# Encoder layer on one core: left operands one piece a round, whole-round weight tiles, a shared subtraction, and a last product in two groups

## The chip, the cores and the metric

One core of a Trainium2 chip runs the whole layer in one launch. The metric is the device time in microseconds (us). The kernel before took 2439.3 us (median of 3 runs, 2437.79 to 2443.6); a measurement of this kernel can tell about 0.3% (7.3 us) from no change.

## What is computed

Two request groups go through one encoder layer with shared weights: the prompt (512 tokens) and the sample (1024 tokens), both of width 1024. Attention and cross-attention are not touched by the change. What is touched is the MLP and the last layer norm:

```python
def squared_relu_mlp(x, w_up, w_down):
    return jnp.square(jax.nn.relu(x @ w_up)) @ w_down
...
        x = layer_norm(ALPHA * x + squared_relu_mlp(x, w_up[l], w_down[l]), ln3_g[l], ln3_b[l])
```

w_up is 1024 x 4096 and w_down 4096 x 1024, all in float32.

## The kernel before

Every float32 product is made of three matmuls in the reduced format F32R: an operand is split into a high part (a cast on ACT) and a low part (the operand minus its high part, a subtraction on POOL or DVE), and high·high, high·low and low·high are summed in one PSUM bank (`mm3`, L128 to L130). A matmul here is 128x128 by 128x512.

The MLP runs in three stages, in this order of time.

The prompt's MLP (1372 to 1772 us of the span) has 32 rounds f. A round makes 128 columns of w_up (`col_block`) and 128 rows of w_down (`down_weights`) into parts, makes 24 matmuls for the hidden block (`up`: ReLU on ACT, square on DVE at L901, cast on ACT, low part on DVE at L904) and 24 for the down product (`down`), whose eight results DVE adds to the tokens (L925). Raw weights come in quarters, 128x512 each, through two shared buffers of the tag `wraw`; their parts lie in three buffers each of the tags `wh` and `wl`. In rounds 3 to 9 a whole call `left(i)` follows the round's own work: it makes one left operand of the sample's MLP, in four pieces k. A piece is an optional sum or difference (DVE, L883), a cast (ACT, L886), a subtraction (DVE, L887) and a store of 512 KB to the DRAM buffer `sa` (L888), through two buffers of the tag `kv`.

The sample's MLP computes each of its two matrix products as a two-by-two block product with seven products in place of eight (`PRODUCTS`: left operand, right operand, and the output blocks to which the result is added or subtracted). The up stage (1772 to 2086 us) runs the seven in the order `UP`, each with 16 blocks f of 12 matmuls; `left_load` brings a left operand back from `sa` (tags qt and pt, or gb and kv); `right` makes the right operand: loads into the tag `q` (seven buffers of 128x528), a sum on DVE (L960) where there are two, a cast on ACT (L963), the subtraction on POOL (L964). DVE adds the results to the hidden blocks (L1001) and squares them (L950). The down stage (2086 us to the end) runs the seven in the order `DOWN`, 16 chunks c of 12 matmuls each (L1045 to L1047, four token tiles by three): the left operand is a hidden block or a sum of two (DVE, L1037), cast on ACT (L1040), subtracted on DVE (L1041); the right operand is `right` with the subtraction on DVE. After a product DVE adds its four banks to the outputs `accs` (L1055, L1057: "collects"). `finish(h)` runs the layer norm on the four token tiles of a half and stores them (L1028): the first half when product 1 is collected, beside the last product, the second half at the end.

In `layer_norm`, L151 and L152 are the statistics, L155 a power on POOL, L159 the first multiplication on DVE. With `spread` 1 both halves of a tile go on with a scaling on ACT (L166) and an addition on POOL (L170); with `spread` 2 the first half is done on DVE (L164) and the second on ACT and DVE (L166, L168).

Each engine works through its own list in order, and so does the queue SP, which issues every DMA. The order of the lists is drawn up when the kernel is built, by the tile framework's planner from program order, buffers and its own estimates, so an instruction may stand earlier in a list than its line says. Buffers of a tag go round in program order.

Of the kernel before, what the change touches and what calls it, by code (L numbers as in the profile page):

```python
# [12 lines left out]
F32 = mybir.dt.float32  # L13
# [7 lines left out]
D = 1024  # L21
# [10 lines left out]
def f32(ap):  # L32
    return ap.bitcast(F32)
# [3 lines left out]
def tile_encoder_layer(ctx: ExitStack, tc: tile.TileContext, d, outs):  # L37
# [109 lines left out]
    def layer_norm(x, g, b, spread=0):  # L147


        st = sb.tile([P, 16], F32, name="lnst", bufs=2)  # L150
        V.bn_stats(st[:, 0:6], x[:, 0:512])  # L151
        V.bn_stats(st[:, 6:12], x[:, 512:1024])  # L152
# [720 lines left out]
    UP, DOWN = (5, 3, 2, 4, 1, 7, 6), (3, 5, 4, 2, 7, 1, 6)  # L873


    def left(i):
        blk = lambda b, k: X2[1 + b[0]][:, 4 * b[1] + k]
        what = PRODUCTS[i][0]
        for k in range(4):
            x = blk(what[0], k)  # L880
            if len(what) > 1:
                y = slot("cpr")
                V.tensor_tensor(y, x, blk(what[2], k), op=what[1])  # L883
                x = y
            t = slot("kv", dt=F32R)
            A.activation(t[:, 0:512], x, AF.Copy)  # L886
            V.tensor_sub(t[:, 512:1024], x, f32(t[:, 0:512]))  # L887
            S.dma_start(sa[i - 1][k], f32(t).rearrange("p (j c) -> p j c", j=2))  # L888
# [65 lines left out]
    def right(what, load, low, tag=None):  # L954
# [7 lines left out]
        t = wp.tile([P, 1024], F32R, name="wh", tag=tag or ("wh", "wl")[next(ring) % 2])  # L962
        A.activation(t[:, 0:512], x, AF.Copy)  # L963
        low.tensor_sub(t[:, 512:1024], x, f32(t[:, 0:512]))  # L964
        return t[:, 0:512], t[:, 512:1024]
# [56 lines left out]
    g3 = None  # L1022

    def finish(h):
        for t in range(4):
            layer_norm(accs[h][t], [g3[:, 0], g3[:, 1]], [g3[:, 2], g3[:, 3]], 1 if t % 2 else 2)
            row = 512 * h + t * P
            S.dma_start(outs[1][0, row:row + P], accs[h][t])  # L1028

    for n, i in enumerate(DOWN):  # L1030
        lw, rw, into = PRODUCTS[i]
        banks = [bank(tag) for tag in (("pj", "pj", "s", "s") if n % 2 == 0 else ("t", "t", "t", "o"))]
        for c in range(16):
            x = hidden(lw[0], c)
            if len(lw) > 1:
                y = wp.tile([P, 512], F32, name="wraw", tag="wraw", bufs=2)
                V.tensor_tensor(y, x, hidden(lw[2], c), op=lw[1])  # L1037
                x = y
            a = wp.tile([P, 1024], F32R, name="wh", tag="wh")
            A.activation(a[:, 0:512], x, AF.Copy)  # L1040
            V.tensor_sub(a[:, 512:1024], x, f32(a[:, 0:512]))  # L1041
            rh, rl = right(rw, down_block(c), V, "wl")
            for t in range(4):
                lh, ll = a[:, t * P:(t + 1) * P], a[:, 512 + t * P:512 + (t + 1) * P]
                T.matmul(banks[t], lh, rh, start=(c == 0), stop=False)  # L1045
                T.matmul(banks[t], lh, rl, start=False, stop=False)  # L1046
                T.matmul(banks[t], ll, rh, start=False, stop=(c == 15))  # L1047
            if n == 0:
                square((1, 1), c)
        for t in range(4):  # L1050
            for b, op in into:
                x = accs[b[0]][t][:, b[1] * 512:(b[1] + 1) * 512]
                if (b, t) not in done:
                    done.add((b, t))
                    V.scalar_tensor_tensor(x, x, ALPHA, banks[t], op0=ALU.mult, op1=op)  # L1055
                else:
                    V.tensor_tensor(x, x, banks[t], op=op)  # L1057
        if i == 7:
            g3 = act.tile([P, 8, 512], F32, name="g3", tag="act")
            for j, name in enumerate(("ln3_g", "ln3_b")):  # L1060
                src = d[name][0]
                S.dma_start(g3[:, 2 * j:2 * j + 2].rearrange("p a c -> p (a c)"),
                            bass.AP(tensor=src.tensor, offset=src.offset, ap=[[0, P], [1, D]]))
        if i == 1:
            finish(0)
    finish(1)


# [62 lines left out]
```

## Time and profile before

| | us |
|---|---|
| median of 3 runs | 2439.3 |
| lowest, highest run | 2437.79, 2443.6 |
| the profiled execution's own time | 2432.93 |
| its span in the trace | 2431.2 |

| engine | busy us | share of the span |
|---|---|---|
| PE (matmul) | 2321.2 | 95% |
| DVE | 1667.1 | 69% |
| ACT | 1034.1 | 43% |
| POOL | 910.0 | 37% |

A matmul's busy time is modelled and matmuls overlap, so the rows are read by the number of matmuls in a stretch and by the pauses between them. Durations of DVE operations overlap a little too: what counts is from start to start.

### The profile page before, as it was taken

How to read it: one execution, taken by the hardware profiler on the slowest of the kernel's cores; microseconds unless marked ns; L12 is line 12 of the kernel's file. 1: busy time of each engine (PE TensorE's matmuls, PEld its weight loads, DVE VectorE, ACT ScalarE, POOL GpSimd, SP SyncE). 2: the span in 40 equal slices, each digit the busy share in tenths (PEclk: the TensorE clock that was granted, in tenths of full speed). 3: DMA queues.
4: the chain of work that ended last, by engine and by line, in shares of the span. 5: the costliest groups of instructions: out<-in, count | busy, mean ns of one | idle time of the engine just before them, and what ended most of it. 6: DMA issues, size and time to landing. Idle time of an engine off the chain costs nothing.

```text
span 2431.2 us, 33241 instructions
## 1 busy us (share of the span) xinstructions
PE 2321.2 (95%) x11128; PEld 1916.6 (79%) x11128; DVE 1667.1 (69%) x3294; ACT 1034.1 (43%) x2181; POOL 910.0 (37%) x798
## 2 busy tenths in 40 slices
PE   8989999999999999999989989999999999999995
PEld 6868778898888787778878876788888877888873
DVE  6266545666656776658576679666655799887997
ACT  4346644666545634434233334333354222344432
POOL 7555442121234125333244444454475445100013
PEclk9999999999999999999999999999999999999998
DMA  9676345444444543435325366433376677634553
GB/s 323 199 191 174 85 119 131 118 115 101 94 119 116 168 130 104 139 113 173 108 92 188 101 205 242 131 98 93 100 242 180 192 240 219 208 125 147 189 170 119
DMA packets 394043, 371.00 MB, mean 153 GB/s; under 512 B 72976, under 2 KB 302352, under 8 KB 393872
## 3 DMA queue, kind: packets, MB, share of 16 engines
q1 hardware_dynamic: 393872, 368.88, 50.7%
q8 instruction: 88, 1.44, 0.2%
q14 instruction: 83, 0.68, 0.1%
HBM read 290.75 MB, written 52.97 MB: 141 GB/s over the span
## 4 chain that ended last, share of the span: by engine, by line
PE 38%; DVE 9%; DMA 4%; issue 3%; POOL 2%; ACT 1%; POOLq 0%; SPq 0%; DVEq 0%; ACTq 0%
PE pj L128 5%; PE pj L129 5%; PE pj L130 5%; DVE cpr L960 2%; PE s L128 2%; PE s L130 2%; PE s L129 2%; PE t L128 2%; PE t L130 2%; PE t L129 2%; PE t L1045 1%; PE t L1046 1%; PE t L1047 1%; DVE h L1001 1%; DMA q<-in_w_up_dram 1%
## 5 line engine op out<-in xcount | busy, mean ns | idle before, releaser
L106 POOL TENSOR_TENSOR wl<-wraw,wh 128x512 fp32r<-128x512 f32 x144 | 196.6, 1378 | 262.8 <-ACT wh L105 240.3
L960 DVE TENSOR_TENSOR cpr<-q 128x512 f32<-128x512 f32 x160 | 148.8, 931 | 47.4 <-DMA q<-in_w_up_dram 19.2
L155 POOL TENSOR_TENSOR lnst<-lnst,mhalf 128x1 f32<-128x1 f32 x48 | 51.6, 1078 | 342.5 <-DVE lnst L154 339.6
L432 ACT ACTIVATE q<-q,st 128x256 f32<-128x256 f32 (+3 forms) x256 | 138.2, 545 | 74.9 <-DVE st L431 72.0
L963 ACT ACTIVATE wh<-cpr 128x512 fp32r<-128x512 f32 x160 | 100.3, 627 | 161.5 <-DVE cpr L960 140.2
L105 ACT ACTIVATE wh<-wraw 128x512 fp32r<-128x512 f32 x144 | 87.9, 629 | 182.3 <-DMA wraw<-in_w_up_dram 50.3
L478 DVE TENSOR_TENSOR pt<-t,pt 128x512 fp32r<-128x512 f32 x160 | 105.4, 671 | 86.5 <-ACT pt L477 85.9
L964 POOL TENSOR_TENSOR wh<-cpr,wh 128x512 fp32r<-128x512 f32 x80 | 114.4, 1431 | 115.7 <-ACT wh L963 115.7
L296 POOL TENSOR_TENSOR wl<-wraw,wh 128x256 fp32r<-128x256 f32 x128 | 95.5, 771 | 153.5 <-ACT wh L295 141.8
L912 POOL TENSOR_TENSOR wl<-wraw,wh 128x512 fp32r<-128x512 f32 x64 | 87.4, 1378 | 122.4 <-ACT wh L911 122.3
L477 ACT ACTIVATE pt<-t 128x512 fp32r<-128x512 f32 x160 | 89.5, 583 | 87.9 <-PE o L490 84.6
L490 PE MATMUL o<-pt,tok 128*128 128x256 f32 (+3 forms) x560 | 114.3, 315 | 5.7 <-ACT q L496 4.3
L925 DVE TENSOR_TENSOR tok<-tok,s 128x512 f32<-128x512 f32 x124 | 83.5, 681 | 41.1 <-PE s L130 41.0
L118 POOL TENSOR_TENSOR wl<-wraw,wh 128x512 fp32r<-128x512 f32 x48 | 62.9, 1324 | 124.9 <-ACT wh L117 124.7
L128 PE MATMUL pj<-x20h,wh 128*128 128x512 f32 x256 | 102.1, 399 | 7.1 <-ACT wh L105 7.0
L925 DVE TENSOR_TENSOR tok<-tok,t 128x512 f32<-128x512 f32 x124 | 83.1, 682 | 31.7 <-PE t L130 31.6
L130 PE MATMUL pj<-x20h,wl 128*128 128x512 f32 x256 | 102.1, 399 | 2.2 <-POOL wl L106 2.1
L129 PE MATMUL pj<-x20l,wh 128*128 128x512 f32 x256 | 101.7, 397 | 0.0
L1040 ACT ACTIVATE wh<-wraw 128x512 fp32r<-128x512 f32 x80 | 50.6, 633 | 119.0 <-issue 40.8
L474 PE MATMUL t<-ident,q 128*128 128x128 f32 x624 | 94.9, 274 | 2.2 <-DVE pt L478 1.0
L490 PEld LDWEIGHTS o<-pt,tok 128*128 128x128 f32 x560 | 83.5, 192 | 11.3 <-ACT q L496 6.2
L428 DVE CUSTOM_DVE_ANT_0 q<-s,gb 128x256 f32<-128x256 f32 (+2 forms) x160 | 67.9, 466 | 27.4 <-PE s L449 21.6
(478 smaller groups left out, 7545.3 us busy)
## 6 DMA issues: line engine op xcount, KB each, us to landing
q<-in_w_up_dram SPq DMA_DIRECT2D x192, 256.0 KB
q<-in_w_down_dram SPq DMA_DIRECT2D x192, 256.0 KB
wraw<-in_w_in_dram SPq DMA_DIRECT2D x96, 256.0 KB
wraw<-in_w_up_dram SPq DMA_DIRECT2D x64, 256.0 KB
wraw<-in_w_down_dram SPq DMA_DIRECT2D x64, 256.0 KB
sa<-kv SPq DMA_DIRECT2D x28, 512.0 KB
kv<-in_c_rope_dram SPq DMA_DIRECT2D x24, 512.0 KB
hd<-qt SPq DMA_DIRECT2D x96, 128.0 KB
```

What stands on the lines that cost most here:

```text
L106: G.tensor_sub(wl[:, sl], r, f32(wh[:, sl]))
L128: T.matmul(out, lh[k], rh[k], start=(k == 0), stop=False, skip_group_check=True)
L129: T.matmul(out, lh[k], rl[k], start=False, stop=False, skip_group_check=True)
L130: T.matmul(out, ll[k], rh[k], start=False, stop=(k == n - 1), skip_group_check=True)
L296: G.tensor_sub(dl, src, f32(dh))
L432: A.activation(p, p, AF.Exp, bias=nm, accum_out=den)
L478: V.tensor_sub(lo[:, 0:x], t[:, 0:x], f32(hi[:, 0:x]))
L490: T.matmul(o[:, q0:q0 + n], v(c, h), part[:, x:x + n], start=(done == 0 and part is hi), stop=(done == total - 1 and part is lo), skip_gro ...
L925: V.tensor_add(x, x, q)
L960: V.tensor_tensor(y, x, z, op=what[1])
L963: A.activation(t[:, 0:512], x, AF.Copy)
L964: low.tensor_sub(t[:, 512:1024], x, f32(t[:, 0:512]))
```

## The change

- `left(i, k)` makes one piece, and rounds 3 to 30 make one each, where rounds 3 to 9 made four each.
- The raw weights of the prompt's MLP come as one 128x1024 tile a block: the up block's through the two buffers of the tag `qt`, the down block's through the two of `pt`.
- In the up stage, the right operand's subtraction goes to DVE, but for odd f of products 1, 4, 7 and 6, where it stays on POOL.
- In the down stage, product 2 moves from the fourth place to the last. It runs in two groups: first token tiles 0 to 2 over all 16 chunks, with the right parts kept in four `act` tiles, then tile 3 over the 16 chunks. The first half's layer norms stand after chunks 3, 7, 11 and 15 of the first group, all with `spread` 1 and with statistics taken earlier (after products 5 and 1); those of tiles 0 to 2 of the second half stand after the second group's matmuls, and tile 3's sums and layer norm (`spread` 2) come last. The gains and biases `g3`, `b3` move from an `act` tile to four of the seven `q` buffers.

```diff
-    def layer_norm(x, g, b, spread=0):
-        st = sb.tile([P, 16], F32, name="lnst", bufs=2)
-        V.bn_stats(st[:, 0:6], x[:, 0:512])
-        V.bn_stats(st[:, 6:12], x[:, 512:1024])
+    def layer_norm(x, g, b, spread=0, st=None):
+        if st is None:
+            st = sb.tile([P, 16], F32, name="lnst", bufs=2)
+            V.bn_stats(st[:, 0:6], x[:, 0:512])
+            V.bn_stats(st[:, 6:12], x[:, 512:1024])
...
-    UP, DOWN = (5, 3, 2, 4, 1, 7, 6), (3, 5, 4, 2, 7, 1, 6)
+    UP, DOWN = (5, 3, 2, 4, 1, 7, 6), (3, 5, 4, 7, 1, 6, 2)
-    def left(i):
+    def left(i, k):
...
+        raw = w_raw(wdn[f * P:(f + 1) * P].rearrange("p (j c) -> p j c", j=2), "pt")
         for ch in range(2):
-            raw = w_raw(wdn[f * P:(f + 1) * P, None, ch * 512:(ch + 1) * 512])[:, 0]
-            A.activation(hi[:, ch], raw, AF.Copy)
-            G.tensor_sub(lo[:, ch], raw, f32(hi[:, ch]))
+            A.activation(hi[:, ch], raw[:, ch], AF.Copy)
+            G.tensor_sub(lo[:, ch], raw[:, ch], f32(hi[:, ch]))
...
-        w, dn = col_block(wup, f * P), down_weights(f)
+        w, dn = col_block(wup, f * P, "qt"), down_weights(f)
         down(up(w), dn, f == 0)
-        if 3 <= f < 10:
-            left(UP[f - 3])
+        if 3 <= f < 31:
+            left(UP[(f - 3) // 4], (f - 3) % 4)
...
-            wh_, wl_ = (x.rearrange("p (k c) -> p k c", k=4) for x in right(what, up_block(f), G))
+            wh_, wl_ = (x.rearrange("p (k c) -> p k c", k=4) for x in right(what, up_block(f), G if i in (1, 4, 7, 6) and f % 2 else V))
...
+    def finish(h, t, spread):
+        layer_norm(accs[h][t], g3, b3, spread, stat.get((h, t)))
+        row = 512 * h + t * P
+        S.dma_start(outs[1][0, row:row + P], accs[h][t])
...
+    for n, i in enumerate(DOWN[:-1]):
...
+        if i in (5, 1):
+            for t in range(4):
+                stats(0, t, 1 if i == 5 else 0)
+    lw, rw, into = PRODUCTS[DOWN[-1]]
+    g3, b3 = ([slot("q", 512) for _ in range(2)] for _ in range(2))
...
+    for c in range(16):
+        if c % 8 == 0:
+            kept.append([act.tile([P, 8, 512], F32R, name="kept", tag="act") for _ in range(2)])
+        rs = right(rw, down_block(c), V, dst=[k[:, c % 8] for k in kept[c // 8]])
+        chunk(banks[0:3], left_parts(lw, c, 0, 3), rs, c)
+        if c % 4 == 3:
+            finish(0, c // 4, 1)
+    for t in range(3):
+        collect(into, t, banks[t])
+    for c in range(16):
+        chunk(banks[3:4], left_parts(lw, c, 3, 4), [k[:, c % 8] for k in kept[c // 8]], c)
+    for t in range(4):
+        if t == 3:
+            collect(into, 3, banks[3])
+        finish(1, t, 2 if t == 3 else 1)
```

`left_parts` makes the sum, the cast and the subtraction of a left block for token tiles t0 to t1 only, `chunk` the three matmuls for each bank given to it.

## Rows read from the trace of the kernel before

**Rows 1.** The page's head and its table of busy time.

```profile
span 2431.2 us, 33241 instructions
PE 2321.2 (95%) x11128; PEld 1916.6 (79%) x11128; DVE 1667.1 (69%) x3294; ACT 1034.1 (43%) x2181; POOL 910.0 (37%) x798
```

**Rows 2.** Windows of the prompt's MLP: stretch, length, busy (count) of PE, PEld, DVE, ACT, POOL.

```profile
1440.00:1576.00 136.00, 122.88 (x496) 95.27 (x495) 106.94 (x149) 52.84 (x89) 59.16 (x42) 0.95 0.59 202
1576.00:1756.00 180.00, 180.00 (x783) 146.61 (x783) 114.06 (x161) 58.24 (x98) 87.75 (x66) 1.00 0.33 98
```

**Rows 3.** L904, one instruction a round: count, ns, first and last start, two windows.

```profile
L904 DVE TENSOR_TENSOR q<-cpr,q x12: 677/680/1777, 1433.0 to 1574.4; 128x512 fp32r<-128x512 f32 x12
...
L904 DVE TENSOR_TENSOR q<-cpr,q x16: 678/693/1798, 1588.5 to 1753.1; 128x512 fp32r<-128x512 f32 x16
```

**Rows 4.** Waits, 1440 to 1576 us: total us, times, longest.

```profile
ACT wh L105 <- DMA wraw<-in_w_up_dram: 19.4, 16, 2.4
ACT kv L886 <- DMA sa<-kv: 18.6, 13, 4.1
PE s L128 <- DVE tok L925: 3.5, 2, 1.9
```

**Rows 5.** Timeline of PE behind one pause: start, duration, idle before and releaser.

```profile
1456.38 0.79 PE L128 MATMUL pj<-x20h,wh 128*128 128x512 f32 x1 [5.44 <-ACT wh L105]
...
1457.83 0.63 PE L129 MATMUL t<-wl,q 128*128 128x512 f32 x1
```

**Rows 6.** Windows of five products of the up stage, from first matmul to first matmul.

```profile
1813.09:1856.65 43.56, 43.56 (x193) 36.03 (x192) 31.71 (x40) 19.89 (x33) 25.12 (x17) 1.00 0.68 207
...
1901.01:1946.11 45.10, 43.73 (x194) 35.88 (x192) 41.82 (x54) 9.99 (x16) 18.65 (x15) 1.00 0.68 206
1946.11:1991.98 45.87, 44.66 (x193) 36.03 (x193) 44.24 (x53) 10.13 (x16) 21.08 (x17) 1.00 0.78 231
1991.98:2039.02 47.04, 43.73 (x193) 35.88 (x192) 46.52 (x50) 10.10 (x16) 24.33 (x16) 0.99 0.73 222
2039.02:2086.24 47.22, 47.22 (x193) 38.19 (x193) 44.67 (x52) 10.56 (x18) 21.73 (x13) 0.94 0.71 220
```

**Rows 7.** Timeline of DVE in the up stage beside one POOL subtraction.

```profile
1925.84 0.68 DVE L1001 TENSOR_TENSOR tok<-tok,pj 128x512 f32<-128x512 f32 x1
1926.55 1.42 DVE L950 SCALAR_TENSOR_TENSOR tok<-tok 128x512 f32<-128x512 f32 x1
```

**Rows 8.** Timeline of POOL at the same place.

```profile
1926.12 1.29 POOL L964 TENSOR_TENSOR wh<-cpr,wh 128x512 fp32r<-128x512 f32 x1 [1.95 <-ACT wh L963]
```

**Rows 9.** L960 in the up stage: ns min, median, max.

```profile
L960 DVE TENSOR_TENSOR cpr<-q x83: 677/817/1793, 1794.4 to 2083.3; 128x512 f32<-128x512 f32 x83
```

**Rows 10.** Windows of the down stage: two products, the last product, what follows it.

```profile
2260.83:2304.87 44.04, 43.81 (x193) 35.96 (x192) 43.20 (x73) 19.18 (x32) 0.00 (x0) 1.00 0.63 208
2304.87:2348.39 43.52, 43.52 (x193) 36.04 (x192) 41.80 (x69) 18.74 (x32) 0.00 (x0) 1.00 0.62 200
2348.39:2410.63 62.24, 47.59 (x188) 36.72 (x187) 52.69 (x92) 21.20 (x34) 20.61 (x8) 0.95 0.35 119
2410.63:2431.20 20.57, 1.32 (x6) 0.75 (x4) 14.59 (x30) 4.11 (x6) 9.81 (x8) 0.66 0.25 102
```

**Rows 11.** Timeline of DVE in the down stage.

```profile
2344.48 0.68 DVE L964 TENSOR_TENSOR wh<-cpr,wh 128x512 fp32r<-128x512 f32 x1
2345.08 0.69 DVE L1037 TENSOR_TENSOR wraw<-tok,h 128x512 f32<-128x512 f32 x1
...
2365.70 1.78 DVE L164 SCALAR_TENSOR_TENSOR qt<-qt,lnst,g 128x512 f32<-128x512 f32 x1
...
2398.24 0.69 DVE L960 TENSOR_TENSOR cpr<-q 128x512 f32<-128x512 f32 x1 [5.07 <-issue]
```

**Rows 12.** DVE groups by shape with narrower tiles: busy us, mean ns.

```profile
L478 DVE TENSOR_TENSOR pt<-t,pt 128x384 fp32r<-128x384 f32 x16 | 8.8, 548 | 1.1 <-ACT pt L477 0.9
...
L382 DVE TENSOR_TENSOR hd<-pj,hd 128x64 fp32r<-128x64 f32 x8 | 1.7, 217 | 0.6 <-ACT hd L381 0.6
```

**Rows 13.** Timeline of POOL beside the last product.

```profile
2363.96 4.66 POOL L170 TENSOR_TENSOR qt<-qt,g 128x512 f32<-128x512 f32 x2 [0.83 <-ACT qt L166]
...
2382.26 12.06 POOL L170 TENSOR_TENSOR pt<-pt,g 128x512 f32<-128x512 f32 x2 [0.83 <-ACT pt L166]
```

**Rows 14.** Waits of the queue SP from 2340 us on.

```profile
SPq L1028 <- POOL pt L170: 10.3, 1, 10.3
SPq L1028 <- POOL qt L170: 7.2, 1, 7.2
```

More of the change, by code (lines that the diff above doesn't have):

```diff
@@ L872, in tile_encoder_layer @@
     }
-    UP, DOWN = (5, 3, 2, 4, 1, 7, 6), (3, 5, 4, 2, 7, 1, 6)
-    def left(i):
-        blk = lambda b, k: X2[1 + b[0]][:, 4 * b[1] + k]
+    UP, DOWN = (5, 3, 2, 4, 1, 7, 6), (3, 5, 4, 7, 1, 6, 2)
+    def left(i, k):
+        blk = lambda b: X2[1 + b[0]][:, 4 * b[1] + k]
         what = PRODUCTS[i][0]
[L879 to L888, printed above, removed]
+        x = blk(what[0])
+        if len(what) > 1:
+            y = slot("cpr")
+            V.tensor_tensor(y, x, blk(what[2]), op=what[1])
+            x = y
+        t = slot("kv", dt=F32R)
+        A.activation(t[:, 0:512], x, AF.Copy)
+        V.tensor_sub(t[:, 512:1024], x, f32(t[:, 0:512]))
+        S.dma_start(sa[i - 1][k], f32(t).rearrange("p (j c) -> p j c", j=2))
     toks[0] = [slot("tok") for _ in range(4)]
@@ L952, in tile_encoder_layer, with right @@
     ring = itertools.count()
-    def right(what, load, low, tag=None):
+    def right(what, load, low, tag=None, dst=None):
         x = load(what[0])
@@ L961, in right @@
             x = y
[L962 to L965, printed above, removed]
+        if dst is None:
+            t = wp.tile([P, 1024], F32R, name="wh", tag=tag or ("wh", "wl")[next(ring) % 2])
+            dst = t[:, 0:512], t[:, 512:1024]
+        A.activation(dst[0], x, AF.Copy)
+        low.tensor_sub(dst[1], x, f32(dst[0]))
+        return dst
     def up_block(f):
@@ L1021, in tile_encoder_layer, with stats, left_parts, chunk @@
     done = set()
[L1022 to L1030, printed above, removed]
+    stat = {}
+    def stats(h, t, ch):
+        if (h, t) not in stat:
+            stat[h, t] = sb.tile([P, 16], F32, name="st", bufs=4)
+        V.bn_stats(stat[h, t][:, 6 * ch:6 * ch + 6], accs[h][t][:, ch * 512:(ch + 1) * 512])
+    def finish(h, t, spread):
+        layer_norm(accs[h][t], g3, b3, spread, stat.get((h, t)))
+        row = 512 * h + t * P
+        S.dma_start(outs[1][0, row:row + P], accs[h][t])
+    def left_parts(lw, c, t0, t1):
+        n = (t1 - t0) * P
+        x = hidden(lw[0], c)[:, t0 * P:t1 * P]
+        if len(lw) > 1:
+            y = wp.tile([P, 512], F32, name="wraw", tag="wraw", bufs=2)[:, 0:n]
+            V.tensor_tensor(y, x, hidden(lw[2], c)[:, t0 * P:t1 * P], op=lw[1])
+            x = y
+        a = wp.tile([P, 1024], F32R, name="wh", tag="wh")
+        A.activation(a[:, 0:n], x, AF.Copy)
+        V.tensor_sub(a[:, 512:512 + n], x, f32(a[:, 0:n]))
+        return [(a[:, j * P:(j + 1) * P], a[:, 512 + j * P:512 + (j + 1) * P]) for j in range(t1 - t0)]
+    def chunk(banks, ls, rs, c):
+        for o, (lh, ll) in zip(banks, ls):
+            T.matmul(o, lh, rs[0], start=(c == 0), stop=False)
+            T.matmul(o, lh, rs[1], start=False, stop=False)
+            T.matmul(o, ll, rs[0], start=False, stop=(c == 15))
+    def collect(into, t, o):
+        for b, op in into:
+            x = accs[b[0]][t][:, b[1] * 512:(b[1] + 1) * 512]
+            if (b, t) not in done:
+                done.add((b, t))
+                V.scalar_tensor_tensor(x, x, ALPHA, o, op0=ALU.mult, op1=op)
+            else:
+                V.tensor_tensor(x, x, o, op=op)
+    for n, i in enumerate(DOWN[:-1]):
         lw, rw, into = PRODUCTS[i]
@@ L1033, in tile_encoder_layer @@
         for c in range(16):
[L1034 to L1047, printed above, removed]
+            ls = left_parts(lw, c, 0, 4)
+            chunk(banks, ls, right(rw, down_block(c), V, "wl"), c)
             if n == 0:
@@ L1050, in tile_encoder_layer @@
         for t in range(4):
[L1051 to L1066, printed above, removed]
+            collect(into, t, banks[t])
[4 more added lines that the diff above has]
+    g3, b3 = ([slot("q", 512) for _ in range(2)] for _ in range(2))
+    for q, name in ((g3, "ln3_g"), (b3, "ln3_b")):
+        for j in range(2):
+            src = d[name][0]
+            S.dma_start(q[j], bass.AP(tensor=src.tensor, offset=src.offset + 512 * j, ap=[[0, P], [1, 512]]))
+    kept = []
+    banks = [bank(tag) for tag in ("pj", "pj", "s", "s")]
+    for c in range(16):
[6 more added lines that the diff above has]
+    for t in range(3):
+        collect(into, t, banks[t])
+    for c in range(16):
[4 more added lines that the diff above has]
+        finish(1, t, 2 if t == 3 else 1)
 def constants():
```

## The prediction

> **What bounds the kernel now.** I read the page's busy table first: PE is busy 95% of the span [rows 1], so only its pauses, and what follows its last matmul, can be won. Then I cut the stretch that the change touches into windows by stage and compared each with a stretch of the same work in which PE never waits.
>
> The prompt's MLP has such a stretch: from 1576 to 1756 us PE is busy throughout [rows 2]. L904 runs once a round. There its 16 starts lie 15 rounds apart, (1753.1 − 1588.5) / 15 = 10.97 us a round; in the rounds with left operands and the few behind them, (1574.4 − 1433.0) / 11 = 12.85 us [rows 3]. So 11 x (12.85 − 10.97) = 20.7 us are lost there. The matmul counts agree: 496 at the steady rate of 180 / 783 = 0.230 us need 114 of the 136 us [rows 2]. The waits name what is late: left pieces wait 18.6 us for their own stores (two `kv` buffers), weight casts wait 19.4 us for quarters in the two `wraw` buffers, and PE waits for DVE's additions, which stand behind the pieces [rows 4]. A pause costs twice: after 5.44 us of idling the matmuls take 0.63 us at the lower clock [rows 5].
>
> In the up stage, a product without loss takes 43.56 us; four of the last ones took 45.10, 45.87, 47.04 and 47.22, 11.0 us over. DVE is what is full there: 177 us busy of 185 [rows 6].
>
> In the down stage the first six products run at about 43.6 us; the last took 62.2, so 18.7 us are lost in it, and 20.6 us follow [rows 10].
>
> **The change part by part.** I number the terms A to D.
>
> *A, the prompt's MLP.* A left piece costs DVE two operations (0.60 us each from start to start [rows 11]), ACT one cast and SP one store of 512 KB. One piece a round brings DVE from 114.06 / 180 x 10.97 = 6.95 us to 8.2 us a round; if each operation also meets a POOL subtraction, which costs it 1.42 − 0.68 = 0.74 us [rows 7], to 9.6. Both are under 10.97, so the pieces lie beside PE's work. A store now has two rounds before its buffer is needed, and the longest wait for one was 4.1 us [rows 4]: none is left. The raw tiles hold two whole rounds where two quarters stood. In steady rounds this is worth nothing, since PE has no idle time to give; in rounds 3 to 14 it guards the casts while stores share the DMA. Both edits work on the same 20.7 us. I take 19: pieces without a sum can be planned early and still bunch (8 of 28). Bounds: 12 (half a microsecond a round of new delay in 17 of the 28 rounds) and 22.
>
> What A moves: the first left operand was loaded into qt and pt during round 4; now it waits for the last raw tiles. Its four loads are 2.1 MB; at the 202 GB/s of the busy window [rows 2] 10.4 us. The last down tile is cast when the parts of the second up block before it come free (three `wh` buffers), some one and a half rounds, 16 us, before the stage ends, so I take 0 and keep 0 to 5. On SP these loads wait behind nothing slow: raw tiles and one store a round.
>
> *B, the up stage.* A POOL subtraction of 1.29 us [rows 8] stops a DVE operation with two SBUF operands: L950 took 1.42 us beside one, where an addition from PSUM takes 0.68 [rows 7]; L960 went up to 1.79 [rows 9], that is +1.1. So a subtraction on POOL costs DVE 0.74 to 1.1 us, and on DVE itself 0.60. In products 4, 1, 7 and 6, 32 of 64 move: DVE gives back 32 x (0.74 to 1.1) = 24 to 35 us and takes 19. Net 5 to 16; I take 8, nearer to the L950 row, which repeats in every block of product 4. DVE then needs 177 − 8 = 169 us beside PE's 4 x 43.56 = 174. From just over PE it comes to just under: I take half of the 11.0 us, 5. In products 5, 3 and 2 all 48 move; DVE is busy only 31.71 of 43.56 us in product 3 [rows 6], and 16 x 0.60 = 9.6 still fit. Bounds: +11, and −4 if each of the 32 moved ones holds DVE for the cast before it (0.63 us on ACT, 20 us in all, which would bring DVE to 189).
>
> *C, the new order of the down products.* A product with sums on both sides has 64 DVE operations a 0.60, 38.4 us, and eight collects 4.8: 43.2, as the row of product 7 shows, and PE keeps 44.0 beside it [rows 10]. Now 7, 1 and 6 follow each other: 43.2, 38.4 + 2.4 = 40.8, and 38.4 + 4.8 + four statistics 2.4 = 45.6, together 129.6 against PE's 130.6. No slack: −1.5, bounds 0 and −5.
>
> *D, the last product and the end.* Before: 62.24 + 20.57 = 82.8 us [rows 10]. After, on PE: 192 matmuls in 43.5 us, and one tile's end behind them. I put this end at 10 us: the 20.57 us behind the last product [rows 10] went to two pairs of tiles one after the other, some 10 a pair, and a single tile's chain is hardly shorter than a pair's. Floor 53.5. On DVE: a 384-column operation takes 0.548 us where 512 columns take 0.69 [rows 11, 12], so 0.46 from start to start; for 128 columns I take 0.20, between the 64-column 0.217 less the same 0.09 overlap and a third of 0.60. Group one: 32 x 0.46 + 16 x 0.60 + 4 collects 2.4 + four norms, each two multiplications a 0.66 and two small ones 0.18, 6.0: 32.7. Group two and the norms of tiles 0 to 2: 6 collects 3.6 + 32 x 0.20 + 3 x (1.5 + two statistics 1.2) = 18.1. Then the end, 10. Sum 60.8.
>
> On top come 14 POOL additions (8 in `finish(0)`, 6 in `finish(1)`). In the last product such additions each held DVE for 1.78 − 0.68 = 1.1 us [rows 11]; with 0.74 at the lower end I take 0.9: 14 x 0.9 = 12.6, less what falls where DVE waits anyway, 9. The Trainium skill, page "SBUF — State Buffer", section "Who interferes with whom", speaks against this part: a DVE instruction with two SBUF inputs and a GpSimd instruction that reads SBUF exclude each other, and the one issued second waits until the first has finished. The trace agrees [rows 7, 8, 13]; taken at its word, each addition would hold DVE for its whole 1.29 us, 18 us, and D would come out 5 us worse.
>
> What D adds as a wait: the four stores of the first half stand in SP's list among the right operand's loads and wait for POOL. Before, two such stores held SP for 7.2 and 10.3 us [rows 14], because POOL's pair of additions took 4.66 and 12.06 us between DVE's [rows 13]; behind them DVE had no load and idled 5.07 us [rows 11]. Now there are four, and with four of the seven `q` buffers taken by g3 and b3 only three loads, some 6 us of work, run ahead. Statistics taken earlier leave the stores less to wait for. Each store costs 0 to 4 us; I take 0 to 1. D is then 60.8 + 9 = 70, a gain of 13. Bounds: 58 (gain 25) and 85 (loss 2).
>
> Sum: 19 + 5 − 1.5 + 13 = 35.5 us, against the profiled execution's 2432.93 us (span 2431.2): 2397. That execution ran 6.4 us under the median of the runs; I take the sum off the median: 2439.3 − 35.5 = 2404.
>
> **The rivals.**
>
> *R1: the last product does not pay.* For it: the SP rows [rows 14], and twice as many stores with fewer loads ahead. Against: only 9 of 82.8 us on DVE need to be hidden. D gives 0: 2404 + 13 = 2417.
>
> *R2: the loss in the prompt's MLP goes by the piece, not by the round.* 28 pieces at 20.7 / 28 = 0.74 us each would keep the whole loss. For it: PE waits for DVE's additions, and DVE works in order [rows 4]. Against: 18.6 us of waiting for stores and the bunching of four pieces go. 2404 + 19 = 2423.
>
> *R3, slower than before: pauses in every round.* Place: rounds 3 to 30. The piece's subtraction waits in DVE's list for a cast that stands behind weight casts on ACT; the additions behind it keep the banks, PE pauses and the clock falls as in [rows 5]. At 2 us a piece 56 us are lost where 20.7 were: 2439.3 + 35 − 16.5 = 2458. It decides from (20.7 + 16.5) / 28 = 1.3 us a piece on. Against: DVE has 1.4 to 2.8 us of slack a round.
>
> *R4: everything in D is hidden and PE sets the pace to the end.* D is 53.5, 16 more: 2388.
>
> **How the numbers follow.** Forecast 0.62, R1 0.18, R2 0.09, R3 0.05, R4 0.06. The predicted time is the forecast's, 2404. Its own bounds, with A's, B's and D's unlikely to fail together, give 2390 to 2418; R1 and R2 take the range to 2424, R4 to 2386. Left out are R3 and R1 and R2 together (2436). A measurement of this kernel can tell about 0.3%, 7.3 us: faster means under 2432. Faster 0.88; same 0.06, mostly R1 and R2 together; slower 0.06, R3 and a late first left operand on top of R1 and R2.
>
> **What would show it.** A: L904 starting every 10.9 to 11.3 us from round 3 to 30, no wait of L886 for `sa`, the clock at 1.00. B: products 4, 1, 7, 6 within 1.5 us of 43.56 on average, and L950 and L960 at 0.69 in even blocks. C: six products in 261 to 266 us. D: 65 to 75 us from the last product's first matmul to the end, SP waits for L170 of at most 5 us each, one tile's store last. Wrong would be: a pause at the first matmul of the up stage (the left operand late), rounds still near 12.85 us (R2), or SP waiting 7 us and more for POOL several times (R1).

## The result, and the profile after

| | us |
|---|---|
| before, median (lowest to highest) beside the changed kernel | 2438.55 (2429.13 to 2443.6) |
| after, median (lowest to highest) | 2409.54 (2404.66 to 2417.2) |
| ratio, with its 95% interval | 0.9888 [0.9846, 0.993] |
| the profiled execution of after, and its span | 2412.69, 2410.9 |

The changed kernel is 1.1% faster: 27 us by the ratio, where 35.5 were forecast. The profiled executions differ by 20.3 us in their spans. Cut at the same matmuls, they differ like this:

| stretch, us | before | after | won |
|---|---|---|---|
| start to the first matmul of the prompt's MLP | 1387.2 | 1390.8 | −3.6 |
| prompt's MLP and first product of the up stage (A) | 425.9 | 411.1 | 14.8 |
| the other six products of the up stage (B) | 273.2 | 263.8 | 9.4 |
| six products of the down stage (C) | 262.2 | 278.5 | −16.3 |
| last down product and what follows (D) | 82.8 | 66.8 | 16.0 |

No edit touches the first stretch; it comes up again at the end. Two lines of the page's head and of its table of busy time, to be read beside [rows 1]: PE's 11128 matmuls are the same as before and its busy time is within 2 us, so what was won is pauses.

```profile
span 2410.9 us, 33078 instructions
PE 2319.2 (96%) x11128; PEld 1916.1 (79%) x11128; DVE 1678.4 (70%) x3400; ACT 1031.0 (43%) x2200; POOL 827.3 (34%) x724
```

**A.** Windows of the prompt's MLP in the kernel after (stretch, length, busy and count of PE, PEld, DVE, ACT, POOL, then PE's clock, DMA share, GB/s), against [rows 2]: in the first 136 us PE now does 565 matmuls, where it did 496.

```profile
1440.00:1576.00 136.00, 132.89 (x565) 106.35 (x564) 94.54 (x138) 47.65 (x85) 69.04 (x46) 0.99 0.45 144
1576.00:1752.00 176.00, 175.81 (x760) 141.95 (x759) 126.07 (x186) 59.97 (x107) 94.41 (x62) 1.00 0.45 144
```

L905 of the kernel after is L904 of before, one instruction a round. Its group in the stretch of the first left pieces (count, least, median and greatest ns, first and last start) answers [rows 3]: 12 rounds in 135.7 us, 11.31 us a round, where it was 12.85.

```profile
L905 DVE TENSOR_TENSOR q<-cpr,q x13: 677/679/1795, 1437.9 to 1573.6; 128x512 fp32r<-128x512 f32 x13
```

The waits of the same stretch (us in total, times, longest) answer [rows 4]. The waits of the casts for `wraw` are gone; the left pieces' wait for their stores is down from 18.6 to 10.6 us, not to none; the additions (L926) still wait for PE's banks.

```profile
DVE tok L926 <- PE t L130: 14.0, 7, 4.0
...
ACT kv L887 <- DMA sa<-kv: 10.6, 4, 5.0
```

**B.** Five products of the up stage in the kernel after, from first matmul to first matmul, against [rows 6]: product 3, then 4, 1, 7 and 6. All run at PE's pace, and DVE is busy 39 to 43 of 44 us in the last four.

```profile
1801.83:1845.40 43.57, 43.57 (x194) 36.04 (x192) 34.87 (x56) 19.41 (x33) 0.00 (x0) 1.00 0.68 203
1889.75:1933.32 43.57, 43.57 (x194) 36.04 (x192) 39.19 (x62) 9.78 (x16) 10.36 (x8) 1.00 0.74 221
1933.32:1977.67 44.35, 44.35 (x194) 36.06 (x192) 43.05 (x63) 10.64 (x17) 10.36 (x8) 1.00 0.82 243
1977.67:2021.24 43.57, 43.57 (x194) 36.04 (x192) 42.41 (x57) 9.49 (x15) 11.85 (x8) 1.00 0.80 239
2021.24:2065.59 44.35, 44.35 (x194) 36.05 (x192) 40.63 (x57) 10.54 (x17) 9.29 (x6) 1.00 0.72 221
```

**C and D.** The down stage in the kernel after, against [rows 10]: products 7, 1 and 6, then group one, group two, and the end. Product 6 takes 59.22 us, and that is the one large loss; its DVE is busy 58.80 of them. Group one runs at PE's pace (144 matmuls, no pause) and leaves DVE 8 us without work.

```profile
2197.23:2241.32 44.09, 43.86 (x194) 35.96 (x192) 43.33 (x73) 19.00 (x32) 0.00 (x0) 1.00 0.58 185
2241.32:2284.84 43.52, 43.52 (x194) 36.04 (x192) 41.80 (x69) 18.71 (x32) 0.00 (x0) 1.00 0.66 200
2284.84:2344.06 59.22, 47.24 (x193) 37.41 (x192) 58.80 (x93) 25.94 (x42) 34.92 (x12) 0.91 0.49 159
2344.06:2376.70 32.64, 32.64 (x145) 27.03 (x144) 24.65 (x49) 14.49 (x28) 0.00 (x0) 1.00 0.29 99
2376.70:2400.10 23.40, 16.34 (x44) 10.01 (x43) 21.80 (x50) 7.84 (x20) 10.64 (x9) 0.71 0.17 67
2400.10:2410.90 10.80, 1.35 (x6) 0.77 (x5) 5.55 (x11) 0.72 (x1) 0.92 (x1) 0.66 0.12 49
```

PE's timeline in product 6 of the kernel after (start, duration, in brackets the idle time before and its releaser): one pause of 10.67 us, from the matmul at 2326.34 to the next, and matmuls of 0.63 us and more behind it, as in [rows 5].

```profile
2326.34 0.39 PE L1052 MATMUL o<-wh 128*128 128x512 f32 x1
2337.01 0.80 PE L1053 MATMUL t<-wh 128*128 128x512 f32 x1 [10.28 <-DVE wh L967]
2337.61 0.63 PE L1054 MATMUL t<-wh 128*128 128x512 f32 x1
```

What stood on DVE ahead of that L967, from DVE's timeline of the same place: eight multiplications L161. They are the layer norms of the first half of the result, which the program has in the last product, behind chunks 3, 7, 11 and 15 of group one.

```profile
2320.23 0.68 DVE L961 TENSOR_TENSOR cpr<-q 128x512 f32<-128x512 f32 x1
2320.84 1.41 DVE L161 SCALAR_TENSOR_TENSOR qt<-qt,st,q 128x512 f32<-128x512 f32 x2
2322.16 2.45 DVE L161 SCALAR_TENSOR_TENSOR pt<-pt,st,q 128x512 f32<-128x512 f32 x2
2324.54 1.78 DVE L1043 TENSOR_TENSOR wraw<-tok,h 128x512 f32<-128x512 f32 x1
2326.24 3.43 DVE L161 SCALAR_TENSOR_TENSOR qt<-qt,st,q 128x512 f32<-128x512 f32 x2
2329.59 3.42 DVE L161 SCALAR_TENSOR_TENSOR pt<-pt,st,q 128x512 f32<-128x512 f32 x2
2332.93 1.75 DVE L961 TENSOR_TENSOR cpr<-q 128x512 f32<-128x512 f32 x1
2334.61 1.75 DVE L1047 TENSOR_TENSOR wh<-wraw,wh 128x512 fp32r<-128x512 f32 x1
2336.28 0.68 DVE L967 TENSOR_TENSOR wh<-cpr,wh 128x512 fp32r<-128x512 f32 x1
```

And POOL at the same place: first the four powers of these norms (one column each), then their eight additions.

```profile
2297.93 21.59 POOL L157 TENSOR_TENSOR st<-st,mhalf 128x1 f32<-128x1 f32 x4 [241.69 <-DVE st L156]
2322.47 3.29 POOL L172 TENSOR_TENSOR qt<-qt,q 128x512 f32<-128x512 f32 x2 [2.96 <-ACT qt L168]
2325.72 3.39 POOL L172 TENSOR_TENSOR pt<-pt,q 128x512 f32<-128x512 f32 x2
2329.08 3.38 POOL L172 TENSOR_TENSOR qt<-qt,q 128x512 f32<-128x512 f32 x2
2332.42 3.38 POOL L172 TENSOR_TENSOR pt<-pt,q 128x512 f32<-128x512 f32 x2
```

The first half's sums are complete once product 1 is collected, so the planner was free to put its norms before the place where the program has them, and it put them into product 6. The multiplications L161 also need the gains `g3`, whose loads SP issues at 2316.5 and 2317.3 us; the first L161 starts at 2320.84. In product 6 DVE has no room. In group one, where it has 8 us, there is nothing left of them.

**The theory after the result.** A and B pay by about what the trace shows; the down changes win 16 us at the end and lose 16 in product 6, because the norms of the first half stand there. Rivals: that one of A and B carries the whole gain and the other none; that A's gain is the pieces' alone; that the loss in product 6 is not the norms', but the new order of the products; that it is POOL's share of the norms.

### The profile page after: what moved, and what is told of

The parts are those of the page before. It is cut to its first block, busy times and chain, and to the rows that moved or that the text cites. A ratio compares the mean times of both kernels' runs of the same rounds, so it can differ in the third digit from the quotient of the medians.

```text
span 2410.9 us, 33078 instructions
## 1 busy us (share of the span) xinstructions
PE 2319.2 (96%) x11128; PEld 1916.1 (79%) x11128; DVE 1678.4 (70%) x3400; ACT 1031.0 (43%) x2200; POOL 827.3 (34%) x724
## 5 line engine op out<-in xcount | busy, mean ns | idle before, releaser
L106 POOL TENSOR_TENSOR wl<-wraw,wh 128x512 fp32r<-128x512 f32 x80 | 107.2, 1355 | 184.3 <-ACT wh L105 158.8
L913 POOL TENSOR_TENSOR wl<-pt,wh 128x512 fp32r<-128x512 f32 x64 | 91.6, 1452 | 120.1 <-ACT wh L912 119.8
L961 DVE TENSOR_TENSOR cpr<-q 128x512 f32<-128x512 f32 x160 | 111.1, 698 | 24.2 <-DMA q<-in_w_up_dram 15.1
L967 POOL TENSOR_TENSOR wh<-cpr,wh 128x512 fp32r<-128x512 f32 x32 | 44.4, 1389 | 228.3 <-ACT wh L966 228.3
L106 POOL TENSOR_TENSOR wl<-qt,wh 128x512 fp32r<-128x512 f32 x64 | 101.7, 1610 | 52.2 <-ACT wh L105 44.4
L926 DVE TENSOR_TENSOR tok<-tok,t 128x512 f32<-128x512 f32 x124 | 82.8, 679 | 37.5 <-PE t L130 37.5
L118 POOL TENSOR_TENSOR wl<-wraw,wh 128x512 fp32r<-128x512 f32 x48 | 63.0, 1327 | 128.8 <-ACT wh L117 125.3
L926 DVE TENSOR_TENSOR tok<-tok,s 128x512 f32<-128x512 f32 x124 | 83.8, 679 | 30.9 <-PE s L130 30.9
L157 POOL TENSOR_TENSOR st<-st,mhalf 128x1 f32<-128x1 f32 x4 | 21.6, 5418 | 241.7 <-DVE st L156 241.7
L1046 ACT ACTIVATE wh<-wraw 128x512 fp32r<-128x512 f32 (+2 forms) x96 | 53.4, 559 | 119.2 <-PE s L1054 30.5
L967 DVE TENSOR_TENSOR wh<-cpr,wh 128x512 fp32r<-128x512 f32 x128 | 95.9, 749 | 9.0 <-ACT wh L966 9.0
```

Source lines behind the costliest of these rows:

```text
L106: G.tensor_sub(wl[:, sl], r, f32(wh[:, sl]))
L926: V.tensor_add(x, x, q)
L967: low.tensor_sub(dst[1], x, f32(dst[0]))
```

## The experiments

The stretches of each experiment's profiled execution, cut like the ones above (down: C and D together):

| kernel | A's stretch | B's stretch | down | ratio to before, 95% interval |
|---|---|---|---|---|
| before | 425.9 | 273.2 | 344.9 | 1 |
| after | 411.1 | 263.8 | 345.3 | 0.9888 [0.9846, 0.993] |
| e1_a | 408.9 | 272.2 | 346.9 | 0.9929 [0.9912, 0.9945] |
| e2_b | 426.3 | 263.8 | 345.3 | 0.9958 [0.9943, 0.9973] |
| e3_cd | 427.4 | 273.2 | 346.6 | 1.0015 [1.0005, 1.0025] |
| e4_ab | 413.0 | 263.8 | 345.4 | 0.9893 [0.9876, 0.991] |
| e5_pieces | 418.6 | 271.6 | 346.3 | 0.9969 [0.9952, 0.9986] |
| e6_raw | 421.6 | 273.3 | 346.1 | 0.9974 [0.9959, 0.9988] |
| e7_fin0 | 409.1 | 263.8 | 343.2 | 0.9882 [0.985, 0.9915] |
| e8_pin7 | 411.4 | 263.8 | 347.6 | 0.9888 [0.9854, 0.9923] |
| e9_nofin | 410.2 | 263.8 | 333.2 | 0.9834 [0.9817, 0.985] |
| e10_allv | 408.4 | 263.7 | 344.1 | 0.9886 [0.9869, 0.9904] |
| e11_ab_fin0 | 408.6 | 263.8 | 340.1 | 0.9871 [0.9854, 0.9887] |
| e12_ord | 409.2 | 263.8 | 346.7 | 0.9898 [0.9884, 0.9913] |

A stretch that an experiment leaves alone repeats within 1 to 5 us, so differences under 2 us in one stretch are not read.

### Each part alone

**e1_a**: the kernel before with both edits of the prompt's MLP.

```diff
-        if 3 <= f < 10:
-            left(UP[f - 3])
+        if 3 <= f < 31:
+            left(UP[(f - 3) // 4], (f - 3) % 4)
...
-        w, dn = col_block(wup, f * P), down_weights(f)
+        w, dn = col_block(wup, f * P, "qt"), down_weights(f)
...
+        raw = w_raw(wdn[f * P:(f + 1) * P].rearrange("p (j c) -> p j c", j=2), "pt")
```

> The kernel before with the two edits of the prompt's MLP alone (one left piece a round, whole-round raw tiles). Theory: the stages add up, so this one is worth what the stage lost in the changed kernel's trace, 385.4 - 370.4 = 15 us from the first up matmul to the up stage: 2424 us by the median of before, ratio 0.994; L904 starts about every 11.1 us from round 3 to 30, and the up stage still takes 314 us. Rival (the prediction's A as put): 19 us, 2420. Rival R2: nothing, because pieces cost by the piece.

Measured: 2415.81 against 2434.06 us, 17.3 us by the ratio, and 17.0 in A's stretch.

**e2_b**: the kernel before with the up stage's subtractions on DVE, but for odd blocks of four products.

```diff
-            wh_, wl_ = (x.rearrange("p (k c) -> p k c", k=4) for x in right(what, up_block(f), G))
+            wh_, wl_ = (x.rearrange("p (k c) -> p k c", k=4) for x in right(what, up_block(f), G if i in (1, 4, 7, 6) and f % 2 else V))
```

> The kernel before with the subtraction's new sharing in the up stage alone. Theory: 9 us (the up stage took 313.6 us before, 304.4 in the changed kernel): 2430, ratio 0.996, every product at 43.5 to 44.4 us. Rival (the prediction's B): half of that, 5 us, with products 7 and 6 still over 45 us; it holds if the changed kernel's up stage was helped by its new MLP stage.

Measured: 2423.24 us, 10.2 us by the ratio, 9.4 in B's stretch. The forecast's 5 is out, and so is any loss.

**e3_cd**: the kernel before with the down changes alone (the changed kernel with the old MLP lines and `right(..., G)`).

> The kernel before with the down stage's changes alone (product 2 last in two groups, norms and statistics moved, g3 and b3 in q). Theory: the changed kernel's down stage took 345.3 us from its first matmul to the end of the span, the kernel before's 345.0, so this is worth 0: 2438, ratio 1.000, with the pause of some 10 us in product 6 and some 16 us saved in the last product and behind it. Rival (the prediction's C and D): -1.5 + 13 = 11.5 us faster, 2427, if the pause was an accident of the other edits' shifts.

Measured: 2437.0 us, ratio 1.0015 [1.0005, 1.0025]. The down changes alone win nothing; by the ratio they cost some 3.7 us. Product 6 has the same pause, 10.67 us from 2352.99 us on.

**e4_ab**: both other parts, with the old down stage.

> The changed kernel with the down stage of the kernel before (both other edits kept). Theory: as fast as the changed kernel, 24 us under before, 2414, ratio 0.990. Rival: the down stage's changes are worth 11.5 us, then this one is 2421 or slower and the changed kernel's gain was partly theirs.

Measured: 2405.84 us, ratio 0.9893, the changed kernel's own within its interval. So A and B carry the whole gain (17.3 + 10.2 = 27.5 alone, 26.0 together), and of the down changes nothing is left. The waits of SP in the last product of e4_ab show what the old order costs, as in [rows 14]:

```profile
SPq L1027 <- POOL pt L170: 10.4, 1, 10.4
SPq L1027 <- POOL qt L170: 7.2, 1, 7.2
```

### Part A, one edit at a time

**e5_pieces**: one left piece a round, raw weights as before. **e6_raw**: whole-round raw tiles, four pieces in rounds 3 to 9 as before. Each is one half of e1_a's diff.

> The kernel before with one left piece a round (rounds 3 to 30) and nothing else; raw weights stay in quarters in two buffers. Theory: the loss of rounds 3 to 9 came from four pieces waiting for two kv buffers and from DVE's list behind them, so the pieces alone give most of the 17 us of both edits: at least 12 us, ratio 0.995 or lower. Rival: the raw quarters were the bound (weight casts waited 19.4 us for them), then the pieces alone give less than 6 us.

> The kernel before with whole-round raw tiles and nothing else; four pieces a round in rounds 3 to 9. Theory: little, 0 to 5 us, ratio 0.998 to 1.000, since the pieces still wait for their stores and hold DVE. Rival: the raw tiles alone give 12 us or more, and PE's pause of some 6 us before the up matmul of round 5 goes.

Measured: 2427.56 us and 2428.39 against 2434.11; A's stretch is 7.3 and 4.3 us shorter. That the pieces alone bring 12 and more was wrong: neither edit has the whole gain. The nine kernels that have both edits are 12.9 to 17.5 us under before in this stretch, against 7.3 + 4.3 = 11.6. By the ratios it is 17.3 against 7.5 + 6.3 = 13.8, with intervals of some 4 us on each, so that the pair brings more than its sum is likely and not shown. The waits say what each edit leaves behind. In the kernel before, two things are late there, stores and raw weights [rows 4]. With the pieces alone (waits of e5_pieces, 1440 to 1576 us) the casts still wait 28 us for raw weights:

```profile
ACT wh L910 <- DMA wraw<-in_w_down_dram: 19.1, 16, 3.6
...
ACT wh L105 <- DMA wraw<-in_w_up_dram: 8.9, 12, 2.0
ACT kv L885 <- DMA sa<-kv: 8.0, 6, 2.7
```

With the raw tiles alone (e6_raw, same stretch) that wait is gone, and the pieces' wait for their stores doubles, from 18.6 to 37.9 us:

```profile
ACT kv L886 <- DMA sa<-kv: 37.9, 15, 6.6
```

Each edit by itself leaves the other's wait in place, or lengthens it.

### Part B, how much of it POOL may keep

**e10_allv**: the changed kernel, with no subtraction of the up stage on POOL.

```diff
-            wh_, wl_ = (x.rearrange("p (k c) -> p k c", k=4) for x in right(what, up_block(f), G if i in (1, 4, 7, 6) and f % 2 else V))
+            wh_, wl_ = (x.rearrange("p (k c) -> p k c", k=4) for x in right(what, up_block(f), V))
```

> The changed kernel with the other 32 subtractions of the up stage on DVE as well, none on POOL. Theory: the up stage is at PE's pace already (its last six products took 263.8 us, 43.97 each), so nothing is left to win: the same within 2 us. Rival: in-order waiting of the DVE subtraction for the cast before it holds DVE; then products 4, 1, 7 and 6, with 4 DVE operations a block and 3.3 us for two blocks' extra, fall behind by 3 us or more in all.

Measured: 2405.28 us; B's stretch 263.7. So sharing the subtractions between POOL and DVE is worth no more than giving DVE all of them; PE's pace is reached either way.

### The down stage: whose are the 16 us in product 6?

**e9_nofin**: the changed kernel without the first half's norms.

```diff
-            finish(0, c // 4, 1)
+            S.dma_start(outs[1][0, c // 4 * P:c // 4 * P + P], accs[0][c // 4])
```

> The changed kernel without the first half's four layer norms: the sums are stored as they are (the statistics are still taken), so this part of the output is left out. It prices the norms where they now stand. Theory: the pause of 10.7 us and most of product 6's other excess is theirs, so the down stage falls from 345.3 to about 331 us and product 6 from 59.2 to about 45. Rival: product 6 is full of its own work (64 operations, 8 collects, 4 statistics, 45.6 us), and g3 and b3 take loads' places: then only 5 us go.

Measured: 2394.89 us; the down stage takes 333.2, so the norms cost 12.1 us. Product 6 in e9_nofin:

```profile
2281.26:2327.05 45.79, 44.47 (x193) 35.73 (x192) 44.82 (x76) 20.31 (x34) 0.00 (x0) 1.00 0.66 219
```

It takes 45.8 us, in the new order of the products and with the loads of `g3` and `b3` still there. Order and loads are cleared; the norms are the cause.

**e7_fin0**: the first half's norms wholly on DVE, without POOL's additions.

```diff
-            finish(0, c // 4, 1)
+            finish(0, c // 4, 0)
```

> The changed kernel with the first half's four layer norms wholly on DVE (no scaling on ACT, no addition on POOL; the four small powers stay on POOL), at the same place in DVE's list. Theory: the pause in product 6 is made by POOL's eight additions, each of which holds DVE's two-operand work (eight multiplications took 11.0 us, 5.3 without contention, and three other operations 1.75 in place of 0.68). Without them DVE does 8 more multiplications (5.3 us) and is spared some 9: product 6 falls from 59.2 to about 55 us, 4 us faster than the changed kernel. Rival: DVE had simply no room there for more work; then 5.3 us more of it lengthens product 6 to about 64 us.

Measured: 2406.64 us; the down stage takes 343.2, 2.1 less than after, which is at the edge of what a stretch can tell. The six products take 274.3 us, 4.2 less, and product 6 takes 55.1, as the theory had it; 2.1 us come back in the last product. DVE's timeline of e7_fin0 shows the exchange: the multiplications L161 now take 0.70 us each where POOL's additions made 1.71 of them, but DVE has eight operations more (L163).

```profile
2316.09 1.41 DVE L161 SCALAR_TENSOR_TENSOR qt<-qt,st,q 128x512 f32<-128x512 f32 x2
...
2325.13 1.41 DVE L163 SCALAR_TENSOR_TENSOR pt<-pt,st,q 128x512 f32<-128x512 f32 x2
```

Eight additions at 1.0 us of DVE's time go, eight operations at 0.66 come: 2.7 us, near the 2.1 measured. Without POOL's additions the norms still cost 10.0 us (343.2 against the 333.2 of e9), so the loss is not POOL's alone. That the additions were cheap does not follow: they cost DVE some 8 us, and DVE needs 5.3 to do their work itself.

**e8_pin7**: gains and biases loaded only behind the eighth chunk of group one, and the norms from there on every second chunk, so that they can't stand so early in product 6.

```diff
+        if c == 7:
+            g3, b3 = ([slot("q", 512) for _ in range(2)] for _ in range(2))
...
-        if c % 4 == 3:
-            finish(0, c // 4, 1)
+        if c >= 7 and (c - 7) % 2 == 0 and (c - 7) // 2 < 4:
+            finish(0, (c - 7) // 2, 1)
```

> The changed kernel with g3 and b3 loaded only after the eighth chunk of the last product's first group, by which the first half's layer norms (same engines: DVE, ACT, POOL) move in DVE's list from the middle of product 6 to its end, where six kept right parts stand ahead. Theory: product 6's pause shrinks from 10.7 us, because its own operands are all made before the norms; the first group had some 8 us of idle DVE time for them. Product 6 at 47 us or less, 5 to 8 us in all faster than the changed kernel. Rival: POOL's additions hold DVE wherever they are, and the same pause of about 10 us shows at the first group's start.

Measured: 2405.74 us; the down stage takes 347.6, 2.3 more than after. The first 6 x 192 matmuls take 265.6 us, 12.9 less than after, but what follows takes 82.0, 15.2 more: PE pauses 3.8, 1.5 and 6.5 us (from one matmul's start to the next) at the start of group one. The last of them in PE's timeline of e8_pin7:

```profile
2341.82 0.79 PE L1052 MATMUL pj<-kept,wh 128*128 128x512 f32 x1 [6.08 <-ACT wh L1046]
```

The cost went along with the norms, as the rival had it; the rival's cause, POOL's additions, is not tested here by itself. The norms still came bunched, the eight L161 in a row from 2319.66 to 2325.03 us, ahead of most of group one's work and not beside it.

**e12_ord**: products 6 and 4 change places, so that product 4 is the one that completes the first half, and the norms are on DVE alone; nothing of them can be ready before group one.

```diff
-    UP, DOWN = (5, 3, 2, 4, 1, 7, 6), (3, 5, 4, 7, 1, 6, 2)
+    UP, DOWN = (5, 3, 2, 4, 1, 7, 6), (3, 5, 6, 7, 1, 4, 2)
...
-        if i in (5, 1):
+        if i in (5, 4):
...
-            finish(0, c // 4, 1)
+            finish(0, c // 4, 0)
```

> The changed kernel with the down products in the order 3, 5, 6, 7, 1, 4, 2, the second statistics after product 4, and the first half's norms wholly on DVE. Product 4 needs 48 DVE operations where 7, 1 and 6 need 64, so it leaves DVE some 10 us in which right parts of the last product can be made ahead (the kept tiles have room), and the norms fall into the first group, where DVE then needs 14.9 + 7.2 + 10.6 = 33 us beside PE's 32.7. Theory: no pause of 10 us anywhere, down stage at 335 to 338 us, 7 to 10 us faster than the changed kernel. Rival: the norms cost their DVE time wherever they stand, as in the run with g3 and b3 loaded late; then the down stage stays at 343 us or more.

Measured: 2408.13 us; the down stage takes 346.7. The sixth product now keeps its pace, 43.5 us, but collects, statistics, norms and the right parts to be kept fall together on DVE in group one's first chunks, with PE pauses of 3.2, 1.7, 2.5, 4.1 and 1.3 us. The sixth product of e12_ord, and the stretch of 49 us behind it:

```profile
2276.62:2320.16 43.54, 43.54 (x193) 36.04 (x192) 35.01 (x57) 20.49 (x37) 0.00 (x0) 1.00 0.60 190
2320.16:2369.00 48.84, 38.37 (x144) 29.44 (x143) 40.64 (x82) 13.74 (x27) 3.95 (x4) 0.90 0.25 88
```

In those 49 us PE does group one, 144 matmuls, for which the changed kernel needs 32.64. DVE is busy 40.64 of 48.84 us, without a pause until 2351 us and waiting for ACT again and again behind that: it has its operations at the wrong time. The rival's number held here too. How much of the 49 us is the norms' is not shown, for there is no run of this order without them.

**e11_ab_fin0**: e4_ab (old down stage), with the first half's norms on DVE alone.

```diff
-            layer_norm(accs[h][t], [g3[:, 0], g3[:, 1]], [g3[:, 2], g3[:, 3]], 1 if t % 2 else 2)
+            layer_norm(accs[h][t], [g3[:, 0], g3[:, 1]], [g3[:, 2], g3[:, 3]], 0 if h == 0 else 1 if t % 2 else 2)
```

> The kernel with the old down stage and both other edits (as in the run with the old down stage), but the first half's norms beside the last product wholly on DVE. Theory: POOL's two pairs of additions held SP for 7.2 and 10.3 us and DVE idled 5.07 us behind them; without them SP's list flows and the last product falls from 62 to about 57 us: 4 to 6 us faster than that run, 2400 us. Rival: DVE alone is the bound there, eight more multiplications cost what the stall gave: no difference.

Measured: 2401.95 us, ratio 0.9871 [0.9854, 0.9887]; the down stage takes 340.1, 5.3 less than e4_ab. SP's stores of the first half no longer wait for POOL, 10.4 and 7.2 us, but for DVE:

```profile
SPq L1027 <- DVE pt L161: 6.6, 2, 5.7
SPq L1027 <- DVE qt L161: 6.6, 2, 5.7
```

In the changed kernel the exchange of eight additions brought 2.1 us; here that of four brings 5.3. SP's two stores of the `pt` tiles took 11.12 us in e4_ab and take 1.67 here, and the 5.22 us that DVE idled in e4_ab behind those stores are gone; that this is the reason is read from the two traces. The kernel has the lowest median of all full kernels, but its interval overlaps those of e7_fin0 and of the changed kernel, so nothing beats the changed kernel beyond doubt.

## Why the prediction was right, and where it was not

The time, 2409.5 us, lies inside the range, 5.5 us above the predicted 2404, and the kernel is faster by more than 0.3%. Two of the four terms carried that; the other two failed as a pair, and B's error hid part of it. That the total came so near is in part luck: A brought 2 to 4 us less than its 19, B 4.4 to 5.2 more than its 5, C and D together 11.9 less than their 11.5, and the 2439.3 from which the sum was taken stands above the medians of 9 and 19 later runs of the same kernel, 2433.4 to 2434.1.

**A: forecast 19, measured 14.8 in the changed kernel and 17 alone. Right.** The rounds take 11.31 us where 10.9 to 11.3 were named, and the clock is at 0.99 to 1.00. The step "none is left", on the waits for stores, was wrong: four waits of together 10.6 us remain, the longest 5.0, although each piece has its own round. The two long ones, 4.9 and 5.0 us, stand before pieces without a sum, which the forecast itself had expected to bunch. The forecast put A together as one term, because both edits work on the same 20.7 us; e5 and e6 show that this was right, as neither edit brings more than some 7 us by itself. No pause stands at the first matmul of the up stage: in the kernel after, PE never idles more than 0.7 us from 1569 us to the end of that stage.

**B: forecast 5, measured 9.4 to 10.2. The mechanism was right, the size was not.** The step that failed is "I take half of the 11.0 us". DVE's need was put at 169 us beside PE's 174; measured were 39.19 + 43.05 + 42.41 + 40.63 = 165, and once DVE fits, nearly the whole loss goes, 9.4 of the 11.0 us, not half of it. That an engine with 5% to spare would still cost half of the pauses had no row behind it.

**C: forecast −1.5, measured −16.3. The failed step is the sum for product 6**, "38.4 + 4.8 + four statistics 2.4 = 45.6". As a sum of what it lists it is right: without the norms product 6 takes 45.8 us (e9). What it leaves out is the work that the forecast put in D, beside group one, because the program has it there. The rows could have said that this is not sure: the lists are the planner's, the norms were ready at the collects of product 1, and nothing that the rows show held them back but the buffers of `g3` and `b3`. With product 6 at 59.2 us the six products took 278.5, where 261 to 266 were named.

**D: forecast 13, measured 16.0, and the agreement means little.** Its size for the norms, 6.0 us of operations and 8 x 0.9 = 7.2 for POOL's additions, is 13.2 against the 12.1 measured by e9. But D's sum counted on group one to take them beside PE. Without them group one is PE's, 32.64 us, with DVE idle for 8 of these; group two and the end took 23.40 + 10.80 = 34.2, where 18.1 + 10 and the rest of the additions gave some 32. C and D belong together: forecast +11.5, measured −0.4, and the 12.1 us of the norms are the difference. They were hidden nowhere. In e8 and e12, which move them to group one's start or behind it, the down stage stays at 347.6 and 346.7 us, 14.4 and 13.5 above e9, and they come in a bunch there.

The addition's price was a question of the page "SBUF — State Buffer" of the Trainium skill, section "Who interferes with whom": a DVE instruction with two SBUF inputs and a GpSimd instruction that reads SBUF exclude each other. The timelines above agree with the exclusion: beside POOL's additions of 1.65 to 1.7 us, DVE's operations take 1.71 to 1.78 us in turn with them, where they take 0.68 alone. That is 1.0 to 1.1 us for an addition, between the 0.9 taken and the whole 1.29.

**The rivals.** R1 put D at 0; D brought 16.0. That the down changes together pay nothing is what e3 and e4 show, and R1's cause for it is not seen in the changed kernel: no store of the first half waits for POOL, and SP's longest wait among the loads is for DVE's own sums (`cpr`, 12.9 us, a load waiting for its `q` buffer). Stores of the second half do wait for POOL, 28.7, 2.2 and 6.1 us, two of them over the 5 us that the forecast allowed, but all loads are issued before them. R1's cause does stand in the old order of the products, where taking POOL out of the first half's norms wins 5.3 us (e11 against e4). R2 is out: the pieces, one a round, bring 7.3 us alone and the rounds go at 11.31. R3 is out: no round has such a pause. R4 is out, as PE waits in product 6 and group two.

**Open.** Whether a place for the norms exists that hides them was not found: spread evenly beside group one, with DVE's 8 us there, was the forecast's picture, and no run had them so.

## What to carry to other kernels

Where a planner draws up the engines' lists, cost a moved step at the earliest place at which its inputs and buffers allow it, not at the line where the program has it: the norms' 12 us fell on a product in which DVE was full already. Where two waits stand in the same rounds, one edit can leave or lengthen the other's wait (7.3 and 4.3 us one by one, 13 to 17 together here), so try the edits together before one is dropped. And an engine that comes from just over its partner's pace to just under it can give back nearly the whole loss: here 9.4 of 11.0 us, where half had been counted.

## What the runs showed of the hardware that was not expected

**One of four one-column powers on POOL took 19.4 us.** In the POOL rows above, the four powers L157 stand as one row of 21.59 us; in e3_cd, e7_fin0 and e8_pin7 they take as long. One by one, in the kernel after, three take 0.6 to 1.0 us and one takes 19.35:

```profile
2299.55 19.35 POOL L157 TENSOR_TENSOR st<-st,mhalf 128x1 f32<-128x1 f32 x1
```

Beside it DVE does one operation with two SBUF operands after another, 0.60 us apart. In e12_ord the powers take about 1 us each, and there too DVE goes on without a pause beside them:

```profile
2333.71 1.40 DVE L161 SCALAR_TENSOR_TENSOR qt<-qt,st,q 128x512 f32<-128x512 f32 x2
2333.87 0.98 POOL L157 TENSOR_TENSOR st<-st,mhalf 128x1 f32<-128x1 f32 x1 [287.55 <-DVE st L156]
2336.53 0.99 POOL L157 TENSOR_TENSOR st<-st,mhalf 128x1 f32<-128x1 f32 x1 [1.67 <-DVE st L156]
```

Nor are those L161, with two SBUF operands each, any longer for it: 1.40 us for two. So a busy DVE is not the whole reason, and what is stays open. The long power was not what put the norms' multiplications so late: L161 does not use the power (in e12_ord the first L161 starts before it), and in the kernel after all four were done at 2319.52 us, 1.3 us before the first L161.

**The unchanged first part differs by up to 13 us from execution to execution.** From the start to the first matmul of the prompt's MLP it took 1379.9 us (e8_pin7) to 1393.2 us (e2_b). The order of the instructions on PE, DVE, ACT and POOL is the same in all fourteen kernels up to some 20 us before that place, and the difference is there already. In the changed kernel, e9_nofin and e10_allv, whose orders are the same to the end of this part, it took 1390.8, 1387.2 and 1385.3 us. Single executions say nothing about a gain of under 13 us in the whole; stretches cut at the same matmuls do better.
